# A decoder layer on one core: its second half recorded and emitted in a planned order, with three plain output pairs, fixed rings, one load queue and earlier gate columns

## The chip, the cores and the metric

The kernel runs on one core of one Trainium2 chip. A core has a matrix engine (PE, with a separate track PEld for its weight loads), a vector engine (DVE), a scalar engine (ACT), a general engine (POOL, used here only to issue transfers) and a queue engine (SP, which only issues transfers). The metric is the device time of one launch in microseconds (us), lower is better. The kernel before was run three times: 2223.91, 2223.79 and 2219.65 us, median 2223.79.

## The reference

One decoder layer for T = 512 tokens, width D = 2048, all inputs fp32. Cut to what matters here:

```python
mod = silu(c) @ W_ada + b_ada            # 6 groups of 16 columns of 128: shift1 scale1 gate1 shift2 scale2 gate2
h   = rms_norm(x) * (1 + scale1) + shift1
u   = h @ W_in                           # conv heads, queries, keys, values, gates
y   = [rms_norm(conv(u)) | rms_norm(attention(u))]
x   = x + gate1 * (y @ W_out)            # attention half of W_out: 8 blobs w_oa, 8 blobs w_oa2
h   = rms_norm(x) * (1 + scale2) + shift2
x   = x + gate2 * (relu(h @ W1)**2 @ W2) # D_FF = 8192
out = rms_norm(x)
```

Three facts follow. The norm of the second `h` needs every column of `x`, so nothing of `h @ W1` can start for a token before the whole output projection of that token is done. gate2 is first needed when `W2` products are added to `x`. The last norm needs every column of the last `x`.

## The kernel before, in words

**Number format.** Each fp32 operand is split in a high part and a rest, and one fp32 product becomes three matmuls (`mm3`, L92 to L95): weight high by token high (L93), weight high by token low (L94), weight low by token high (L95). A weight blob of 128x1024 fp32 (0.5 MB) is loaded by SP into the raw ring `rw` of 6 tiles (`raw_blob`, L790), its high part made by an ACT copy (L800) and its low part by a DVE subtract (L801) into the ring `hl` of 3 tiles (`hilo`, `hl_tile`). Token tensors are kept transposed, 128 channels by tokens.

**What orders the work.** All instructions go through a tile framework that schedules them when the kernel is built; each engine then runs its own list in that order. The first part of the kernel is pinned to its program order through `pin` (`keep_in_program_order`). From the output projection `w_oa` on, nothing is pinned and the framework's scheduler decides. Tiles come from rings whose owner is also decided there: a main pool of 29 slots (`slot`), 5 temporaries (`temp`), 2 accumulators (`accum`), and 8 PSUM banks of 512 fp32 (`bankf`).

**Gate and shift columns.** A column of `mod` is two 0.5 MB blobs of `W_ada`, each multiplied with silu(c) by one DVE instruction (`dot`, L132 to L134; `ada`, L142). 56 columns stand in a list `todo` (L254) that is worked off inside the projections and the attention. The last 8 columns of gate2 are done in the loop over the `w_oa` blobs: `ada(M_G2 * NK + 8 + k, raw_blob)`, 16 loads and 16 dots.

**Output projection.** The loop over `w_oa` takes 8 blobs, each into 8 banks, 512 tokens wide. Then the 8 blobs of `w_oa2` are kept split (`kept`, L834) and `late_out(hf)` (L848) computes 8 x 8 x 3 matmuls of 256 tokens for the low half of the tokens, later for the high half. `residual` (L812) adds the result to `x`, and `square_into` gathers the squares for the norm. `low_tokens` (L888) norms the low half and makes the token operands B1 and B2; `row_norm` (L168) and `high_tokens(q)` (L897) do the high half.

**First feed-forward matrix.** 32 output pairs `p`; one pair is two 128-channel outputs for 512 tokens, from four blobs of `w_f1`. It is computed by a seven-product Strassen-Winograd scheme: `operands` (L918) makes three new weight sums and splits seven operands; each product is a `run` (L941) of 24 matmuls of 256 tokens against one of seven token operands B1, U6, T5, B2, T7, B3, T4. `ff1(p)` (L971) combines the results with five DVE subtracts from PSUM, squares, makes the seven operands of the hidden activations and stores them to DRAM tensors `gd` (L1015 and L1019, on POOL). Between the output projection and the loop over the pairs, `ahead` (L962) does the B1 and B2 products of pairs 0 to 2, which need low tokens only, while the high tokens are made.

**Second matrix.** For each of 8 groups `f` the seven token operands are read back from `gd` (14 loads of 512 KB, L1121, on POOL); 4 groups `q` of four `w_f2` blobs each are multiplied in the same seven-product scheme. In the first group the residual `x` is also read back in eight loads (`residual_pairs`, L1082, on POOL). `update` (L1046), `final` (L1051) and `finish` (L1056) add to `x` and norm it; the last quarter `plain(3)` (L1091) is done with eight ordinary products so that the end can be norming one half while the other is computed.

The order of the region, as written:

```python
    late_out(0); low_tokens(); late_out(1)
    ahead(0, B1); row_norm(bankf, sacc, D, r2, 2, 4)
    ahead(1, B1); high_tokens(0); ahead(2, B1); high_tokens(1)
    ahead(0, B2); high_tokens(2); ahead(1, B2); ahead(2, B2); high_tokens(3)
    for p in range(32): ff1(p)
    for f in range(8):            # L1117: 14 token loads, then 4 (in the last group 3) groups of blobs
        ...
    plain(3)
```

Of the kernel before, what the change touches and what calls it, by code (L numbers as in the profile page):

```python
# [8 lines left out]
F32 = mybir.dt.float32  # L9
# [27 lines left out]
M_SH1, M_SC1, M_G1, M_SH2, M_SC2, M_G2 = range(6)  # L37


@with_exitstack  # L40
def hybrid_layer(ctx: ExitStack, tc: tile.TileContext, a, out):
# [126 lines left out]
    def row_norm(bank, square, width, dst, t0=0, t1=NQ):  # L168
        total = bank()
        for t in range(t0, t1):  # L170
            nc.tensor.matmul(total[:, t:t + 1], square[:, t * P:(t + 1) * P], ones[:, 0:1],
                             start=True, stop=True)
        row_bcast(bank, total[:, t0:t1], width, dst[:, t0 * P:t1 * P])
# [73 lines left out]
    for i in range(4):  # L247
# [7 lines left out]
        + [M_G2 * NK + k for k in range(8)]  # L255
# [526 lines left out]
    HT = T // 2  # L782
    LO, HI = slice(0, HT), slice(HT, T)
# [3 lines left out]
    def bankf():  # L787
        return psf.tile([P, T], F32, name="pf")

    def raw_blob(src):  # L790
        raw = ffp.tile([P, 1024], F32, name="rw", bufs=6)
# [3 lines left out]
    def hl_tile():  # L795
        t = ffp.tile([P, 2, 1024], F32R, name="hl", bufs=3)
        return t[:, 0], t[:, 1]

    def hilo(dst, src):
        nc.scalar.activation(dst[0], src, AF.Copy)  # L800
        nc.vector.tensor_tensor(out=dst[1], in0=src, in1=dst[0].bitcast(F32), op=OP.subtract)  # L801
        return dst
# [9 lines left out]
    def residual(ps, m, c):  # L812
        xm = x1[m // 2][:, m % 2, c]
        nc.vector.scalar_tensor_tensor(out=xm, in0=ps[:, c], scalar=col(M_G1, m), in1=xm,
# [8 lines left out]
    for k in range(8):  # L823
# [4 lines left out]
        ada(M_G2 * NK + 8 + k, raw_blob)  # L828
    for i in range(8):
        residual(pm[i], i, whole)  # L830
# [4 lines left out]
    for i in range(8):  # L835
        if i < 3:
            dst = hl_tile()
        elif i == 3:
            dst = [ffp.tile([P, 1024], F32R, name="sg", bufs=2) for _ in range(2)]
        elif i == 4:  # L840
            dst = [ffp.tile([P, 2, 2, HT], F32R, name="gt", bufs=3).rearrange("p a b c -> p (a b c)")
# [4 lines left out]
    pm = [bankf() for _ in range(8)]  # L846

    def late_out(hf):  # L848
        c = halves[hf]
        for i in range(8):  # L850
            wh, wl = kept[i]
            for k in range(8):
                s = slice(k * P, (k + 1) * P)
                mm3(pm[i][:, c], wh[:, s], wl[:, s], mixa[k][:, 0, c], mixa[k][:, 1, c], k == 0, k == 7)
            residual(pm[i], 8 + i, c)
# [31 lines left out]

    def low_tokens():  # L888
        row_norm(bankf, sacc, D, r2, 0, 2)
# [7 lines left out]
    def high_tokens(q):  # L897
        xs2 = [x1[2 * q], x1[2 * q + 1]]
        for j in range(2):
            normed(2 * q + j, 1)  # L900
        t5, t7 = temp((P, 2, HT), name="t5"), temp((P, 2, HT), name="t7")
        for j, x in enumerate(xs2):
            sub(t5[:, j], x[:, 0, LO], x[:, 0, HI])
            sub(t7[:, j], x[:, 0, HI], x[:, 1, HI])
        for i, t in ((T5, t5), (T7, t7)):
            tok[i][q] = tslot()
            tsplit(tok[i][q], t)
        u6, t4 = temp((P, 2, HT), name="u6"), temp((P, 2, HT), name="t4")
        tok[B3][q] = tslot()
        for j, x in enumerate(xs2):  # L910
            sub(u6[:, j], t5[:, j], x[:, 1, HI], OP.add)
            sub(t4[:, j], x[:, 1, LO], u6[:, j])
            split(tok[B3][q][:, j], x[:, 1, HI])
        for i, t in ((U6, u6), (T4, t4)):
            tok[i][q] = tslot()
            tsplit(tok[i][q], t)

    def operands(raw, only=None):  # L918

        a11, a21, a22, a12 = raw  # L920
        s1, s2 = [ffp.tile([P, 1024], F32, name="sg", bufs=2) for _ in range(2)]
        sub(s1, a21, a22, OP.add)
        sub(s2, s1, a11, OP.add)
        skip = only is not None
        if not skip:
            yield hilo(hl_tile(), a11)
        else:
            yield None
        yield hilo(hl_tile(), s2)
        yield hilo(hl_tile(), s1)  # L930
        if not skip:
            yield hilo(hl_tile(), a12)
        else:
            yield None
# [318 lines left out]
```

## Time and profile before

| | us |
|---|---|
| median of three runs | 2223.79 |
| the profiled execution | 2224.19 |
| its span, first to last instruction | 2222.4 |
| PE busy in it | 2131.6 |
| DVE busy | 1918.1 |
| ACT busy | 1008.2 |
| POOL busy | 193.6 |
| mean granted PE clock | 0.981 of full |

The profile is that of one execution. Its page gives busy times, the span in 40 slices, the chain of work that ended last, and groups of instructions by line and operands. A matmul's own duration (0.28 us for 256 tokens) overlaps its neighbours, so the pace of PE is read from the count in a stretch, not from the mean of one. The stages of the region that the change touches lie, in the span's time, at: `w_oa` 797 to 842.4, `late_out(0)` and most of `late_out(1)` 842.4 to 892.9, the way into the pairs 892.9 to 975, the pairs to 1559.8, the way into the second matrix to 1600, the groups `f` to 2140, the last quarters to 2206.95, and the end to 2222.4.

### The profile page before, as it was taken

The page shows a single profiled execution, that of the slowest core. Times are in us where ns is not written, and L with a number is a line of the kernel's source. Part 1 is how long each engine was busy: PE and PEld are TensorE (multiplying, and loading weights), DVE is VectorE, ACT ScalarE, POOL GpSimd, SP SyncE. Part 2 cuts the span into 40 slices and gives each one's busy share as a digit, 9 for nine tenths or more (in the row PEclk, how much of TensorE's full clock was granted, in tenths as well). Part 3 has the DMA queues.
Part 4 walks back from the last instruction along what each step waited for, and adds up shares of the span by engine and source line. Part 5 has one row for each costly group of instructions (what it writes and reads, how often), then busy time and mean ns, then how long its engine had stood idle before and what let it go on. Part 6 is the DMA issues. An engine that isn't in the chain of part 4 may idle for free.

```text
span 2222.4 us, 37637 instructions
## 1 busy us (share of the span) xinstructions
PE 2131.6 (96%) x14942; PEld 1969.9 (89%) x14942; DVE 1918.1 (86%) x2998; ACT 1008.2 (45%) x1468; POOL 193.6 (9%) x366
## 2 busy tenths in 40 slices
PE   6999989999999999799999999999899999999997
PEld 4777778898777779799999999999899999999996
DVE  8889978877496687999999999999799999999996
ACT  4431333222354435665666556666333333333353
POOL 0000000000000001021111111113211011011000
PEclk7999999999999999899999999999999999999998
DMA  8985686954211165276665666658865466366442
GB/s 343 336 323 180 237 313 256 356 216 180 86 39 57 57 266 185 81 233 209 199 196 195 199 211 196 201 190 283 296 241 195 157 237 233 119 237 235 151 146 95
DMA packets 143984, 453.61 MB, mean 204 GB/s; under 512 B 15809, under 2 KB 20161, under 8 KB 143809
## 3 DMA queue, kind: packets, MB, share of 16 engines
q1 hardware_dynamic: 91104, 322.22, 40.4%
q0 software_dynamic: 51616, 127.95, 17.2%
q8 instruction: 117, 1.92, 0.3%
q10 hardware_dynamic: 1088, 1.05, 0.1%
q14 instruction: 59, 0.48, 0.1%
HBM read 383.00 MB, written 68.16 MB: 203 GB/s over the span
## 4 chain that ended last, share of the span: by engine, by line
PE 75%; DVE 13%; ACT 5%; DMA 4%; issue 2%; SPq 0%; DVEq 0%; ACTq 0%; POOL 0%; POOLq 0%
PE pf L95 18%; PE pf L93 18%; PE pf L94 18%; PE ps L94 5%; PE ps L95 5%; PE ps L93 5%; DVE scr L134 3%; DVE wl L84 2%; DMA tk<-g 1%; DVE hl L801 1%; ACT wh L83 1%; PE pw L94 1%; PE pw L95 1%; PE pw L93 1%; PE pt L719 1%
## 5 line engine op out<-in xcount | busy, mean ns | idle before, releaser
L93 PE MATMUL pf<-tk,hl 128*128 128x256 f32 x3576 | 1008.0, 282 | 12.3 <-DMA tk<-g 6.0
L95 PE MATMUL pf<-tk,hl 128*128 128x256 f32 x3576 | 1005.5, 282 | 12.2 <-DVE hl L801 12.2
L94 PE MATMUL pf<-tk,hl 128*128 128x256 f32 x3576 | 1006.7, 282 | 1.3 <-DVE tk L872 1.3
L93 PEld LDWEIGHTS pf<-tk,hl 128*128 128x128 f32 x3576 | 678.2, 190 | 15.3 <-ACT hl L800 8.0
L95 PEld LDWEIGHTS pf<-tk,hl 128*128 128x128 f32 x3576 | 676.7, 190 | 14.8 <-DVE hl L801 14.7
L94 PEld LDWEIGHTS pf<-tk,hl 128*128 128x128 f32 x3576 | 677.0, 189 | 1.7 <-DVE tk L872 1.6
L800 ACT ACTIVATE hl<-rw 128x1024 fp32r<-128x1024 f32 x264 | 278.8, 1056 | 303.6 <-PE pf L95 254.9
L801 DVE TENSOR_TENSOR hl<-rw,hl 128x1024 fp32r<-128x1024 f32 x264 | 321.9, 1219 | 25.6 <-ACT hl L800 25.2
L800 ACT ACTIVATE hl<-sg 128x1024 fp32r<-128x1024 f32 x189 | 200.3, 1061 | 267.7 <-PE pf L95 242.9
L801 DVE TENSOR_TENSOR hl<-sg,hl 128x1024 fp32r<-128x1024 f32 x189 | 230.5, 1221 | 41.7 <-ACT hl L800 41.3
L134 DVE SCALAR_TENSOR_TENSOR scr<-wa,cs 128x1024 bf16<-128x1024 f32 x176 | 211.0, 1220 | 8.1 <-DMA wa<-in_w_ada 8.0
L83 ACT ACTIVATE wh<-raw 128x1024 fp32r<-128x1024 f32 (+1 forms) x105 | 110.8, 1059 | 221.0 <-PE ps L94 105.1
L84 DVE TENSOR_TENSOR wl<-raw,wh 128x1024 fp32r<-128x1024 f32 (+1 forms) x105 | 128.6, 1225 | 56.6 <-ACT wh L83 54.2
L875 DVE TENSOR_TENSOR sg<-sg,rw 128x1024 f32<-128x1024 f32 x126 | 153.5, 1219 | 0.9
L95 PE MATMUL ps<-h_m,wl 128*128 128x512 f32 x360 | 142.8, 397 | 2.5 <-DVE wl L84 2.4
L93 PE MATMUL ps<-h_m,wh 128*128 128x512 f32 x360 | 142.6, 396 | 2.4 <-ACT wh L83 1.2
L94 PE MATMUL ps<-h_m,wh 128*128 128x512 f32 x360 | 141.8, 394 | 0.0
L1049 DVE SCALAR_TENSOR_TENSOR x<-pf,mod,x 128x256 f32<-128x256 f32 x256 | 119.7, 479 | 17.9 <-PE pf L95 14.9
L93 PE MATMUL ps<-h,wh 128*128 128x512 f32 x280 | 113.2, 404 | 13.1 <-ACT wh L83 9.1
L95 PE MATMUL ps<-h,wl 128*128 128x512 f32 x280 | 113.7, 406 | 2.4 <-DVE wl L84 2.4
L94 PE MATMUL ps<-h,wh 128*128 128x512 f32 x280 | 113.3, 405 | 0.0
L1015 POOL DMA_DIRECT2D g<-gt x192 | 101.0, 532 | 86.4 <-DVE gt L872 81.2
(325 smaller groups left out, 2974.1 us busy)
## 6 DMA issues: line engine op xcount, KB each, us to landing
rw<-in_w_f SPq DMA_DIRECT2D x262, 512.0 KB, 4.3
wa<-in_w_ada SPq DMA_DIRECT2D x176, 512.0 KB, 6.2
tk<-g POOLq DMA_DIRECT2D x114, 512.0 KB, 8.1
g<-gt POOLq DMA_DIRECT2D x192, 256.0 KB, 5.0
raw<-in_w_conv SPq DMA_DIRECT2D x32, 512.0 KB, 6.6
raw<-in_w_kv SPq DMA_DIRECT2D x16, 512.0 KB, 5.4
raw<-in_w_cv SPq DMA_DIRECT2D x16, 512.0 KB, 4.5
raw<-in_cmp_w SPq DMA_DIRECT2D x16, 512.0 KB, 5.4
```

Source lines behind the costliest of these rows:

```text
L83: pin(nc.scalar.activation(wh[:, :cols], raw[:, :cols], AF.Copy))
L84: pin(nc.vector.tensor_tensor(out=wl[:, :cols], in0=raw[:, :cols], in1=wh[:, :cols].bitcast(F32), op=OP.subtract))
L93: pin(nc.tensor.matmul(ps, lh, rh, start=start, stop=False, skip_group_check=more))
L94: pin(nc.tensor.matmul(ps, lh, rl, start=False, stop=False, skip_group_check=more))
L95: pin(nc.tensor.matmul(ps, ll, rh, start=False, stop=stop, skip_group_check=more))
L134: pin(nc.vector.scalar_tensor_tensor(out=scr, in0=w, scalar=1.0, in1=cs[i].rearrange("p a b -> p (a b)"), op0=OP.mult, op1=OP.mult, accum_ ...
L719: nc.tensor.transpose(pt[:, r * P:(r + 1) * P], probs[b, r][:, kb * P:(kb + 1) * P], ident)
L800: nc.scalar.activation(dst[0], src, AF.Copy)
L801: nc.vector.tensor_tensor(out=dst[1], in0=src, in1=dst[0].bitcast(F32), op=OP.subtract)
L875: nc.vector.tensor_tensor(out=dst, in0=x, in1=y, op=op)
L1015: nc.gpsimd.dma_start(out=gd[p // 4][idx[j]][p % 4 // 2][:, p % 2], in_=g[:, j])
L1049: nc.vector.scalar_tensor_tensor(out=xm, in0=src, scalar=gate, in1=xm, op0=OP.mult, op1=OP.add)
```

## The change

1. **Recorded order.** A class `Order` stands in for `nc` from `w_oa` on. It records every call with its operands, derives dependences from their extents, and gives each instruction a cost. `emit` then keeps PE's program order except for instructions marked `floating` (the norms), works due times back from the products, and simulates the five engines to pick at each step the instruction that can start earliest, among equals the one due first. All instructions go out in the order of their simulated begins, pinned.
2. **Fixed rings.** Every ring of the region becomes a `cycle` over tiles taken once, so owners follow the recorded order. In the second matrix two of the five temporaries and the tile `spare` hold `base`.
3. **Gate columns.** All 16 gate2 columns stand in `todo`. The eight that left the `w_oa` loop are worked off in the query projections; of their 16 loads six stand on SP ahead of the first `w_oc` blobs.
4. **Late output projection.** Two blobs share one PSUM bank, so a half takes 4 banks and not 8.
5. **Three plain pairs.** Pairs 0, 1 and 2 are computed with eight ordinary runs each and not with seven: 12 runs on the low tokens, then 12 on the high tokens. `plan`, `makes` and `stay` fix which blob is split when; five of the 24 operands are kept from the low part, so 19 blobs are loaded and split. `results_of` combines with two PSUM adds for a pair and not five. `ahead` and `snapshot` go.
6. **High tokens.** `high_tokens` first makes T5 and B3 for all four quarters, then T7, U6 and T4. T5 has its sign turned, so the weight operand s1 is split with a minus (`hilo(..., minus)`).
7. **One load queue.** The token loads from `gd` and the loads of the residual move from POOL to SP. The stores stay on POOL.
8. **Finish.** `finish` becomes one function whose norm is `floating`.

The diff at its core:

```diff
+class Order:
+    RATE = 390e3
...
+    def emit(self):
...
+                for x in c:
+                    at = max(free[e], x.ready, wire - 2.0 if x.size else 0.0)
...
+                    key = (at, 0 if x.loose else 1, x.late, x.i)
...
+        for x in sorted(out, key=lambda x: (x.begin, x.i)):
+            self.tc.keep_in_program_order(x.call())
...
-        + [M_G2 * NK + k for k in range(8)]
+        + [M_G2 * NK + k for k in range(NK)]
...
+    nc = order = Order(tc, x1[0].tensor.tag, NMAIN)
+    rw = cycle([ffp.tile([P, 1024], F32, name="rw", bufs=6) for _ in range(6)])
+    hl = cycle([ffp.tile([P, 2, 1024], F32R, name="hl", bufs=3) for _ in range(3)])
...
+    banks = cycle([psf.tile([P, T], F32, name="pf") for _ in range(8)])
+    temps = cycle([temp() for _ in range(5)])
...
-    def hilo(dst, src):
+    def hilo(dst, src, minus=False):
+        if minus:
+            nc.scalar.activation(dst[0], src, AF.Copy, scale=-1.0)
+            nc.vector.scalar_tensor_tensor(out=dst[1], in0=src, scalar=-1.0, in1=dst[0].bitcast(F32),
+                                           op0=OP.mult, op1=OP.subtract)
...
-        ada(M_G2 * NK + 8 + k, raw_blob)
...
     def late_out(hf):
+        ps = []
         for i in range(8):
+            if i % 2 == 0:
+                ps.append(bankf())
...
-                mm3(pm[i][:, c], wh[:, s], wl[:, s], mixa[k][:, 0, c], mixa[k][:, 1, c], k == 0, k == 7)
+                mm3(ps[-1][:, halves[i % 2]], wh[:, s], wl[:, s], mixa[k][:, 0, halves[hf]],
+                    mixa[k][:, 1, halves[hf]], k == 0, k == 7)
...
+    def half_norm(hf, dst):
+        with floating():
+            row_norm(bankf, sacc, D, dst, 2 * hf, 2 * hf + 2)
...
+    NP = 3
+    plan = [(p, b, i, u, 0, i == B1) for p in range(NP)
+            for b, i, u in ((A11, B1, 0), (A21, B1, 1), (A12, B2, 0), (A22, B2, 1))]
...
+    def results_of(p):
+        xy, zv = [next(rw) for _ in range(2)]
...
+            sub(y[:, 1 - u], firsts[p, u], results[p, u][:, HI], OP.add)
...
     late_out(0)
+    half_norm(0, r2)
     low_tokens()
     late_out(1)
-    ahead(0, B1)
-    row_norm(bankf, sacc, D, r2, 2, 4)
...
-    for p in range(32):
+    for n in range(5):
+        make(n)
+    for n in range(12):
+        part(n)
+    half_norm(1, r2)
+    high_tokens()
+    for n in range(12, 24):
+        part(n)
+        if n in (17, 19, 23):
+            results_of({17: 2, 19: 0, 23: 1}[n])
+    for p in range(NP, 32):
         ff1(p)
...
     def finish(hf):
         c = halves[hf]
+        with floating():
+            ps = row_norm(bankf, sacc, D, rf, 2 * hf, 2 * hf + 2)
...
-            nc.gpsimd.dma_start(out=x1[k], in_=x1d[k])
+            nc.sync.dma_start(out=x1[k], in_=x1d[k])
...
-                nc.gpsimd.dma_start(out=tok[i][j], in_=gd[f][i][j])
+                nc.sync.dma_start(out=tok[i][j].bitcast(F32), in_=gd[f][i][j].bitcast(F32))
...
     plain(3)
+    order.emit()
```

More of the change, by code (lines that the diff above doesn't have):

```diff
@@ L920, in operands @@
+    def operands(raw, minus=False):
         a11, a21, a22, a12 = raw
[L921 removed]
+        s1, s2 = [next(sg["sums"]) for _ in range(2)]
         sub(s1, a21, a22, OP.add)
         sub(s2, s1, a11, OP.add)
[L924 to L928, printed above, removed]
[L929 to L934 removed]
+        yield hilo(hl_tile(), a11)
+        yield hilo(hl_tile(), s2)
+        yield hilo(hl_tile(), s1, minus)
+        yield hilo(hl_tile(), a12)
```

399 lines of the change are left out of this document (290 added, 109 removed).

## The prediction, as recorded before the changed kernel ran

> **What bounds the kernel now.** I read the page's busy times first, then the stages, then groups and waits in the stages that lose time.
>
> ```profile
> PE 2131.6 (96%) x14942; PEld 1969.9 (89%) x14942; DVE 1918.1 (86%) x2998; ACT 1008.2 (45%) x1468; POOL 193.6 (9%) x366
> PE 75%; DVE 13%; ACT 5%; DMA 4%; issue 2%; SPq 0%; DVEq 0%; ACTq 0%; POOL 0%; POOLq 0%
> ```
>
> PE is busy 96% of the span, so an order can only win what PE loses. The last line is the chain that ended last: 75% matmuls, 13% DVE. Where PE loses is told by stretches (columns: stretch, length, busy time and count of PE, PEld, DVE, ACT, POOL, granted clock, DMA share, GB/s):
>
> ```profile
> 520.00:590.00 70.00, 70.00 (x304) 56.73 (x303) 36.02 (x45) 24.72 (x33) 0.00 (x0) 1.00 0.26 91
> 797.00:842.40 45.40, 41.78 (x178) 33.33 (x179) 36.65 (x59) 12.42 (x15) 1.21 (x2) 1.00 0.87 336
> 842.40:892.90 50.50, 49.92 (x416) 49.32 (x414) 39.12 (x75) 29.11 (x62) 6.48 (x10) 1.00 0.46 162
> 892.90:975.00 82.10, 67.20 (x467) 63.48 (x467) 78.89 (x131) 49.95 (x83) 7.94 (x15) 0.88 0.44 143
> 975.00:1559.80 584.80, 584.80 (x4966) 584.80 (x4965) 537.82 (x717) 361.98 (x509) 116.73 (x222) 1.00 0.66 210
> 1559.80:1600.00 40.20, 31.80 (x247) 31.04 (x246) 29.05 (x39) 11.90 (x15) 9.95 (x19) 0.92 0.93 342
> 1600.00:2140.00 540.00, 540.00 (x4582) 540.00 (x4581) 498.71 (x692) 209.83 (x211) 51.07 (x95) 1.00 0.55 199
> 2140.00:2206.95 66.95, 62.82 (x513) 61.04 (x511) 57.26 (x102) 33.61 (x62) 0.00 (x0) 1.00 0.19 63
> 2206.95:2222.40 15.45, 2.07 (x9) 1.06 (x7) 7.45 (x15) 2.38 (x6) 0.00 (x0) 0.62 0.61 209
> ```
>
> The fifth row gives the pace: 584.8 / 4966 = 0.1178 us a 256-token matmul with PE never idle, so a run of 24 is 2.83 us. At that pace the 416 and 467 matmuls before 975 would take 49.0 and 55.0 us; they lose 1.5 and 27.1 us. Of the 27.1 PE stands still for 14.9; the rest is the clock of 0.88. In the same way 1559.8 to 1600 loses 40.2 - 29.1 = 11.1, and 2140 to 2206.95 loses 66.95 - 60.4 = 6.5. The two long middles lose nothing. So some 46 us can be won, and no more unless work goes.
>
> **The change part by part.** *Gate columns out of the w_oa loop.* Sixteen dots go:
>
> ```profile
> L134 DVE SCALAR_TENSOR_TENSOR scr<-rw,cs x16: 1218/1221/1227, 800.1 to 830.6; 128x1024 bf16<-128x1024 f32 x16
> L93 PE MATMUL pf<-mixa,hl 128*128 128x512 f32 x48 | 19.0, 395 | 2.2 <-ACT hl L800 2.2
> L95 PE MATMUL pf<-mixa,hl 128*128 128x512 f32 x48 | 19.0, 396 | 0.5 <-DVE hl L801 0.5
> L95 PE MATMUL pf<-mixa,wl 128*128 128x512 f32 x16 | 5.5, 402 | 1.3 <-DVE wl L84 1.3
> ...
> 783.58 17.46 SPq L792 DMA_DIRECT2D rw<-in_w_ada  x4
> ...
> raw<-in_w_q SPq DMA_DIRECT2D x16, 512.0 KB, 3.6
> ```
>
> They are 16 x 1.22 = 19.5 us of DVE. Moved to the query projections they meet 70 - 36 = 34 us of idle DVE in the row from 520 to 590, with a DMA share of 0.26, so they cost nothing there. The tightest place in the changed lists: one gate load on SP waits for PE, its dot stands ahead of the last query weight's rest on DVE, and the first w_oc blobs stand behind it on SP. Load, dot and rest are 3.6 + 1.22 + 1.22 = 6.0 us after that wait; PE has two more blobs to do by then, 48 of the matmuls that run at 70 / 304 = 0.23 us, 11 us. If that cover were gone it would cost up to 6. In the w_oa loop PE waited 2.2 us for the first split, whose blob stood behind the four gate loads on SP quoted last but one, and 0.5 us for its rest. The load now comes earlier, but its split tile lies on staging tiles that earlier products still read, so I take 1.0 of the 2.7 (bounds 0 and 3). **-1.0.**
>
> *From the output projection into the pairs (842.4 to 975).* The groups of PE that wait, and what DVE does there:
>
> ```profile
> L95 PE MATMUL pf<-tk,hl 128*128 128x256 f32 x159 | 48.8, 307 | 9.2 <-DVE hl L801 9.2
> L93 PE MATMUL pf<-tk,hl 128*128 128x256 f32 x162 | 50.0, 309 | 2.7 <-ACT hl L800 2.1 <-DVE gy L875 0.4
> L171 PE MATMUL pf<-ones,sacc 128*128 128x1 f32 x8 | 1.2, 255 | 1.7 <-DVE sacc L810 1.7
> L94 PE MATMUL pf<-tk,hl 128*128 128x256 f32 x162 | 48.8, 302 | 1.3 <-DVE tk L872 1.3
> ...
> L801 DVE TENSOR_TENSOR hl<-rw,hl 128x1024 fp32r<-128x1024 f32 x15 | 18.3, 1220 | 1.3 <-ACT hl L800 1.2
> L875 DVE TENSOR_TENSOR gy<-pf,gy 128x256 f32<-128x256 f32 x5 | 2.1, 419 | 0.0
> ```
>
> PE waits 9.2 us for weight rests, 2.7 for high parts, 1.7 for the norm's sums, 1.3 for tokens: DVE is the bound, with 39.1 + 78.9 = 118 us busy of 132.6. The plain pairs take DVE work off: 19 splits in place of 21 splits and 12 weight sums are 14 fewer at 1.22 = 17.1 us; two PSUM adds and not five, three times, are 9 at 0.42 = 3.8. DVE is left with about 98 us. They cost PE three runs more: 72 x 0.1178 = **+8.5**. PE then needs (49.0 + 55.0) + 8.5 = 112.5 us; DVE fits with 15 to spare. ACT loses two copies and was the bound nowhere. The half norm floats:
>
> ```profile
> 894.79 0.61 PE L171 MATMUL pf<-ones,sacc 128*128 128x1 f32 x4 [1.68 <-DVE sacc L810]
> ...
> 896.63 1.03 PE L197 MATMUL pf<-dg,ones 128*128 128x256 f32 x2
> ...
> 2206.92 0.28 PE L95 MATMUL pf<-tk,sg 128*128 128x256 f32 x1
> 2209.48 0.61 PE L1060 MATMUL pf<-ones,sacc 128*128 128x1 f32 x4 [2.28 <-DVE sacc L810]
> ```
>
> The sums waited 1.68 us with PE empty; in the changed program's list they stand 15 products (1.8 us) behind the last product of the late output projection. Today the sums start 2.56 us behind the last product at the very end (2206.92 to 2209.48), and at least 1.7 here, so up to 0.8 us of wait stays in each of two norms, and about as much at the broadcast. One new wait: the scratch of `results_of` takes two of the six raw tiles, so the second and third blob of the fourth pair may be late by up to one run, 2.8 us. Losses left: 3 us in the sum; the lower bound is 0, the upper 12 (the 9.2 us of weight rests and the new wait, all staying). 28.6 - 3 = **-25.6.**
>
> Four banks a half and the turned sign move no time: the minus keeps one ACT and one DVE instruction of the same width, under a PE that is never idle in the pairs; a DVE form slower by as much as the dot against the subtract (1221 against 1220) is nothing.
>
> *Into the second matrix (1559.8 to 1600).* The waits of 1540 to 1600, and POOL's list:
>
> ```profile
> PE pf L93 <- DMA tk<-g: 6.0, 2, 5.4
> POOL g L1019 <- DVE gb L90: 4.8, 1, 4.8
> PE pf L95 <- DVE hl L801: 2.4, 2, 2.0
> ...
> 1553.69 0.54 POOL L1019 DMA_DIRECT2D g<-gb  x1 [4.85 <-DVE gb L90]
> 1554.22 0.54 POOL L1121 DMA_DIRECT2D tk<-g  x1
> ...
> 1563.12 1.21 POOL L1121 DMA_DIRECT2D tk<-g  x2 [0.92 <-DMA tk<-g]
> ```
>
> POOL issues token loads between stores, and a store that waits for its split (4.85 us) holds the loads behind it; PE waited 5.4 us for one. On SP the loads pass the stores. They then share the queue with weight blobs, and on average the stage already moves 342 GB/s at a share of 0.93, so the transfers themselves could be late: 14 loads and eight residual loads of 512 KB are 11.5 MB, 34 us at that rate. Token slots come free from 17 us ahead of the turn, and not all seven operands are needed first; I leave 1 us (bounds 0 and 11.1). **-10.1.**
>
> *The groups f.* The seven turns between groups lost nothing while POOL carried the loads. POOL's waits, over the span, and the loads:
>
> ```profile
> POOL tk L1121 <- PE pf L95: 487.9, 51, 61.3
> rw<-in_w_f SPq DMA_DIRECT2D x262, 512.0 KB, 4.3
> tk<-g POOLq DMA_DIRECT2D x114, 512.0 KB, 8.1
> ```
>
> A token load waits for its slot, up to 61.3 us, and on POOL nothing hurried stood behind it. On SP weight blobs do. The planned list puts each load where its slot should be free and the six raw tiles cover 1.5 groups of four blobs, 29.7 us at 7 x 2.83 = 19.8 a group; I take **0**, and its other end is a rival.
>
> *The last quarters (2140 to 2206.95).* PE's waits there:
>
> ```profile
> ACT hl L800 <- DVE rw L875: 12.3, 2, 6.4
> PE pf L93 <- ACT hl L800: 3.4, 3, 1.3
> ```
>
> A weight sum reaches DVE late, ACT waits 6.4 us for it, and PE waits 3.4 us for high parts. Due times put such sums first; I take half of the 6.5 lost: **-3.5** (bounds -6.5 and +5, a wait of ACT's size passed to PE). Behind 2206.95 the chain of last square, sum, norm, scaling and stores stays: 0.
>
> **Sum**: -1.0 - 25.6 + 8.5 - 10.1 - 3.5 = -31.7. Span 2222.4 - 31.7 = 2190.7; 1.8 us lie around it (2224.19 against 2222.4), so 2192.5. The profiled execution is 0.4 above the median of the runs, so 2192 by the median.
>
> The clock matters to what waits are left. Between 892.9 and 975 PE stood 14.9 us and lost 27.1, 1.8 for each us. [...]
>
> **The rivals.** *Slower: the fixed lists fall out of step in the pairs and groups.* Today the long middles have slack that the framework's own order keeps. Ten pairs, 1200 to 1400:
>
> ```profile
> L801 DVE TENSOR_TENSOR hl<-rw,hl 128x1024 fp32r<-128x1024 f32 x41 | 50.1, 1221 | 3.7 <-ACT hl L800 3.7
> L801 DVE TENSOR_TENSOR hl<-sg,hl 128x1024 fp32r<-128x1024 f32 x30 | 36.6, 1221 | 7.2 <-ACT hl L800 7.2
> ```
>
> DVE is 92% busy (537.82 of 584.80) and waits 3.7 + 7.2 = 10.9 us for ACT in ten pairs. The planner prices a 1024-wide subtract at 1.13 us where it takes 1.22, so its list can put work ahead of a split that then is late by a little each time. The gain of 31.7 is gone when 60 pairs and groups lose 0.53 us each. If the 1.1 us that DVE waits per pair passed to PE, 60 x 1.1 = 66 us, the time is 2258. Against it: 1.6 us of slack per pair and a ring of three operands, 5.7 us ahead of PE. Chance 0.08. [...]
>
> *Slower: the one load queue.* A token load on SP whose slot is not yet free stops the blobs behind it; it decides when such a wait passes the 29.7 us cover, and at seven turns a wait like the 61.3 us seen on POOL costs 7 x (61.3 - 29.7) = 221 us, one of 36 us costs 7 x 6.3 = 44, which makes 2236. For it: POOL waited 487.9 us in 51 waits. Against: the loads are listed by when the slots free. Chance 0.05.
>
> *The way into the pairs keeps half its loss.* If late norms and scratch hold 11 us and more, with the clock: 2192 + 11 = 2203. For it: 19 loads and splits must be timed right against DVE's remaining 98 us. Chance 0.13. *The turn to the second matrix keeps its loss* since DMA is at 0.93 there: 2192 + 10 = 2202. Chance 0.10. *All of it goes*, the leftovers of 1 + 3 + 3 and the last of w_oa too: 2183. Chance 0.10. *The order does not do what it says*, each wait taking a new place at the old size: 2224, chance 0.04.
>
> **How the numbers follow.** The likeliest case, 2186 to 2198 about 2192, has 0.50. Faster takes 0.50 + 0.13 + 0.10 + 0.10 = 0.83; slower 0.08 + 0.05 and half of the last case, 0.15; same 0.02 (0.2%, about what a measurement of this kernel can tell from no change). The range leaves out the slower rivals and a little of the two partial cases together (2192 + 11 + 10 = 2213) and of the best: 2180 to 2214.
>
> **What would show it.** Right: about 116 us where 132.6 were between 842.4 and 975 with DVE below 90% and the clock near 1; a turn to the second matrix with PE waiting under 2 us and no POOL token load; PE never idle in the pairs. Wrong: PE waiting on weight rests in every pair, or on raw blobs at each turn of `f` with SP waiting on token slots; a wait of 3 us or more before the fourth pair.

## The result and the profile after

The changed kernel took 2209.98 us (median of four runs, 2207.75 to 2211.31) where the kernel before took 2223.85 in the same session: a ratio of 0.9941, 95% interval 0.9923 to 0.9958. It is 13.9 us faster. The forecast was 31.7 us faster; the sign was right, the time lies inside the range, and the gain is less than half of what was said.

The page of the changed kernel gives these totals and this chain that ended last. All instructions of the recorded region carry line 111, the line that records a call; the first part's lines have moved (L93, L94, L95 are L286, L287, L288, and L84 is L277).

```profile
span 2206.0 us, 37901 instructions
PE 2134.1 (97%) x15014; PEld 1975.4 (90%) x15014; DVE 1896.1 (86%) x2975; ACT 1007.3 (46%) x1469; POOL 128.2 (6%) x244
PE 81%; DVE 10%; DMA 4%; ACT 3%; issue 1%; SPq 0%; DVEq 0%; ACTq 0%
```

PE has its 72 more matmuls, DVE 22 us less work than the 1918.1 of before, as reckoned. The stretches of the changed kernel (columns as in the prediction):

```profile
788.60:800.00 11.40, 7.32 (x21) 5.44 (x20) 7.10 (x11) 2.68 (x4) 0.00 (x0) 0.70 0.40 144
800.00:843.60 43.60, 42.11 (x174) 33.35 (x173) 16.36 (x16) 14.79 (x16) 0.67 (x1) 0.96 0.44 155
843.60:892.40 48.80, 47.07 (x392) 46.35 (x391) 35.90 (x68) 27.07 (x58) 6.33 (x10) 1.00 0.42 152
892.40:964.00 71.60, 70.51 (x593) 69.83 (x592) 59.76 (x113) 49.53 (x89) 9.16 (x17) 1.00 0.46 151
964.00:985.00 21.00, 16.06 (x115) 15.56 (x114) 15.59 (x20) 9.17 (x13) 2.63 (x5) 0.84 0.53 167
985.00:1148.70 163.70, 162.98 (x1380) 162.60 (x1379) 149.38 (x198) 99.49 (x138) 29.55 (x56) 1.00 0.64 204
1148.70:1502.70 354.00, 354.00 (x3002) 354.00 (x3001) 323.87 (x431) 219.80 (x307) 64.93 (x123) 1.00 0.62 198
1502.70:1625.50 122.80, 119.92 (x1002) 119.75 (x1001) 109.30 (x148) 60.41 (x81) 14.75 (x28) 0.99 0.85 304
1625.50:2098.80 473.30, 473.30 (x4002) 473.30 (x4002) 435.84 (x596) 177.30 (x167) 0.00 (x0) 1.00 0.52 198
2098.80:2191.65 92.85, 92.85 (x784) 92.74 (x782) 89.18 (x157) 51.12 (x90) 0.00 (x0) 1.00 0.35 128
```

The reader is to see that the way into the pairs is now nearly full (70.51 of 71.60) but for one hole at 964 to 985, that the last quarters have none, and that a new hole stands at the very start of the `w_oa` stage, with the clock at 0.70.

To compare like with like I cut both traces at the same products: the first and last `w_oa` product, the last product of the late output projection, and then products counted from the last one (8776, 5776, 4776 and 776 before it), which are the same work in both. Times in us, each the difference of two starts in the trace's timeline; the last column is the kernel with four edits, told below.

```
stage                                  forecast   before    after   four edits
start to first w_oa product               0       793.2    788.6     790.9
w_oa                                     -1.0      49.1     54.9      47.5
late output projection          }       -17.1      47.7     48.9      46.3
way in, to 8776 before the last }                 263.7    256.3     247.5
3000 products of the pairs                0       353.4    354.1     354.5
1000 products, the turn                 -10.1     129.2    122.8     118.3
4000 products of the groups               0       471.7    473.3     473.1
last 776 products                        -3.5      98.9     92.7      92.6
end                                       0        15.5     14.5      14.8
```

The first row can't be put down to the change: the 1601st matmul, ahead of every instruction that the change touches, starts at 404.2 in the trace before and at 401.5 in the trace after, and over the experiments, with and without the moved gate columns, the first `w_oa` product starts anywhere from 788.6 to 791.7. So the profiled spans (16.4 us apart) show a little more than the medians (13.9). What is missing of the forecast lies mainly in three rows: `w_oa` 5.8 us longer and not 1.0 shorter, the way into the pairs with the late projection 6.3 shorter and not 17.1, the turn 6.4 and not 10.1. The last quarters gave 6.2 and not 3.5.

The waits of PE from `w_oa` to the last product, of the changed kernel:

```profile
PE pf L111 <- ACT hl L111: 7.3, 3, 3.4
PE pf L111 <- DVE wl L277: 4.1, 1, 4.1
PE pf L111 <- DVE hl L111: 2.0, 2, 1.5
PE pf L111 <- DVE x L111: 1.7, 3, 0.6
PE pf L111 <- ACT rw L111: 0.9, 2, 0.5
```

The longest of them have an experiment each below. The kernel before had 13.1 us for weight rests in twelve waits and 6.0 for token loads:

```profile
PE pf L95 <- DVE hl L801: 13.1, 12, 3.1
PE pf L93 <- ACT hl L800: 7.7, 6, 2.2
PE pf L93 <- DMA tk<-g: 6.0, 2, 5.4
```

### The profile page after: what moved, and what is told of

It is laid out like the page before. It is cut to its first block, busy times and chain, and to the rows that moved or that the text cites. A ratio compares the mean times of both kernels' runs of the same rounds, so it can differ in the third digit from the quotient of the medians.

```text
span 2206.0 us, 37901 instructions
## 1 busy us (share of the span) xinstructions
PE 2134.1 (97%) x15014; PEld 1975.4 (90%) x15014; DVE 1896.1 (86%) x2975; ACT 1007.3 (46%) x1469; POOL 128.2 (6%) x244
## 4 chain that ended last, share of the span: by engine, by line
PE 81%; DVE 10%; DMA 4%; ACT 3%; issue 1%; SPq 0%; DVEq 0%; ACTq 0%
PE pf L111 62%; PE ps L287 5%; PE ps L288 5%; PE ps L286 5%; DVE scr L327 3%; DVE wl L277 2%; ACT wh L276 1%; DMA wa<-in_w_ada 1%; PE pw L288 1%; PE pw L287 1%; PE pw L286 1%; PE pt L912 1%; DMA raw<-in_w_conv 1%; PE pv L286 1%; PE pv L287 0%
## 5 line engine op out<-in xcount | busy, mean ns | idle before, releaser
L111 PE MATMUL pf<-tk,hl 128*128 128x256 f32 x10704 | 1272.3, 282 | 9.0 <-ACT hl L111 6.3
L111 PEld LDWEIGHTS pf<-tk,hl 128*128 128x128 f32 x10704 | 1269.8, 189 | 10.4 <-ACT hl L111 6.7
L111 ACT ACTIVATE hl<-sg 128x1024 fp32r<-128x1024 f32 x180 | 191.0, 1061 | 260.0 <-PE pf L111 242.7
L327 DVE SCALAR_TENSOR_TENSOR scr<-wa,cs 128x1024 bf16<-128x1024 f32 x192 | 229.9, 1220 | 7.3 <-DMA wa<-in_w_ada 7.0
L111 DVE TENSOR_TENSOR hl<-sg,hl 128x1024 fp32r<-128x1024 f32 x151 | 184.7, 1223 | 36.3 <-ACT hl L111 36.2
L277 DVE TENSOR_TENSOR wl<-raw,wh 128x1024 fp32r<-128x1024 f32 (+1 forms) x105 | 128.7, 1226 | 41.0 <-ACT wh L276 40.2
L111 DVE SCALAR_TENSOR_TENSOR x<-pf,mod,x 128x256 f32<-128x256 f32 (+1 forms) x280 | 135.0, 488 | 19.0 <-PE pf L111 18.2
L111 DVE TENSOR_TENSOR sg<-sg,rw 128x1024 f32<-128x1024 f32 x120 | 146.1, 1218 | 0.0
L288 PE MATMUL ps<-h_m,wl 128*128 128x512 f32 x360 | 142.9, 397 | 2.4 <-DVE wl L277 2.4
L286 PE MATMUL ps<-h_m,wh 128*128 128x512 f32 x360 | 142.8, 397 | 2.1 <-ACT wh L276 1.9
L287 PE MATMUL ps<-h_m,wh 128*128 128x512 f32 x360 | 142.0, 394 | 0.0
L286 PE MATMUL ps<-h,wh 128*128 128x512 f32 x280 | 113.4, 405 | 12.3 <-ACT wh L276 8.8
L288 PE MATMUL ps<-h,wl 128*128 128x512 f32 x280 | 113.7, 406 | 2.5 <-DVE wl L277 2.4
L287 PE MATMUL ps<-h,wh 128*128 128x512 f32 x280 | 113.2, 404 | 0.0
L288 PEld LDWEIGHTS ps<-h_m,wl 128*128 128x128 f32 x360 | 67.8, 188 | 20.7 <-DVE wl L277 5.1
L111 DVE TENSOR_TENSOR sg<-rw 128x1024 f32<-128x1024 f32 x60 | 73.2, 1220 | 13.9 <-DMA rw<-in_w_f 11.5
L286 PEld LDWEIGHTS ps<-h_m,wh 128*128 128x128 f32 x360 | 67.8, 188 | 18.9 <-ACT wh L276 4.1
L287 PEld LDWEIGHTS ps<-h_m,wh 128*128 128x128 f32 x360 | 67.7, 188 | 15.5
```

Source lines behind the costliest of these rows:

```text
L111: x.i, x.eng, x.call = len(self.nodes), eng, (lambda: real(*args, **kw))
L277: pin(nc.vector.tensor_tensor(out=wl[:, :cols], in0=raw[:, :cols], in1=wh[:, :cols].bitcast(F32), op=OP.subtract))
L286: pin(nc.tensor.matmul(ps, lh, rh, start=start, stop=False, skip_group_check=more))
L287: pin(nc.tensor.matmul(ps, lh, rl, start=False, stop=False, skip_group_check=more))
L288: pin(nc.tensor.matmul(ps, ll, rh, start=False, stop=stop, skip_group_check=more))
L327: pin(nc.vector.scalar_tensor_tensor(out=scr, in0=w, scalar=1.0, in1=cs[i].rearrange("p a b -> p (a b)"), op0=OP.mult, op1=OP.mult, accum_ ...
```

## The experiments

### The written order of the first w_oa products

The start of the `w_oa` stage in PE's timeline, kernel before:

```profile
793.21 0.40 PE L93 MATMUL pf<-mixa,wh 128*128 128x512 f32 x1
...
796.17 0.39 PE L94 MATMUL pf<-mixa,wh 128*128 128x512 f32 x1
797.88 0.50 PE L95 MATMUL pf<-mixa,wl 128*128 128x512 f32 x1 [1.32 <-DVE wl L84]
...
799.61 0.39 PE L93 MATMUL pf<-mixa,wh 128*128 128x512 f32 x1
```

and after:

```profile
788.62 0.62 PE L111 MATMUL pf<-mixa,wh 128*128 128x512 f32 x2
793.33 0.79 PE L111 MATMUL pf<-mixa,wl 128*128 128x512 f32 x1 [4.08 <-DVE wl L277]
```

Before, the framework's scheduler had put 14 of the 16 products with the high part of the first blob ahead of the first with its rest (793.21 to 796.56); those of the last bank came behind seven products with the rest, at 799.61. The recorded order keeps the products as `mm3` writes them, so the third product needs the rest, which DVE makes behind the last steps of the attention's output. The experiment puts the high products ahead, for this one blob, and all 16 of them:

```diff
         for i in range(8):
             s = slice(i * P, (i + 1) * P)
-            mm3(pm[i], wh[:, s], wl[:, s], mixa[k][:, 0], mixa[k][:, 1], k == 0, k == 7)
+            if k:
+                mm3(pm[i], wh[:, s], wl[:, s], mixa[k][:, 0], mixa[k][:, 1], False, k == 7)
+            else:
+                nc.tensor.matmul(pm[i], wh[:, s], mixa[k][:, 0], start=True, stop=False)
+                nc.tensor.matmul(pm[i], wh[:, s], mixa[k][:, 1], start=False, stop=False)
+        if k == 0:
+            for i in range(8):
+                nc.tensor.matmul(pm[i], wl[:, i * P:(i + 1) * P], mixa[k][:, 0], start=False, stop=False)
```

> The changed kernel, but for the first w_oa blob the 16 products with the weight's high part go ahead of the eight with its rest, as the scheduler had them before. Theory: keeping the written order of the products puts a product with the rest third in the list, so PE waits 4.1 us for the rest and then runs some 3.4 us at half clock; with 16 products (3.7 us) ahead of it the wait and the slow clock go: the stretch from the first to the last w_oa product falls from 54.9 us to 49 to 50, the time from 2210 to about 2205. Rival: the splits of the next blobs bound the stage anyway, the wait only moves to them: 0 to 1.5 us, 2208.5 to 2210.

Measured: 2203.66 us (2201.03 to 2208.22), ratio to before 0.9914 [0.9899, 0.9928]. Its `w_oa` stage and PE's start in it:

```profile
789.70:837.20 47.50, 45.21 (x193) 35.59 (x192) 23.32 (x27) 17.28 (x20) 0.67 (x1) 1.00 0.52 176
...
789.65 3.88 PE L111 MATMUL pf<-mixa,wh 128*128 128x512 f32 x16
794.34 1.88 PE L111 MATMUL pf<-mixa,wl 128*128 128x512 f32 x7 [0.81 <-DVE wl L277]
```

The wait is 0.81 us and not 4.08, the clock of the stage is 1.00, and the stage is 47.5 us and not 54.9. That is 7.4 us, of which the waits for the rest are 3.3; the others come with the clock (0.70 and 0.96 in the two rows of the changed kernel). By the median it is 6.3. The theory holds; the waits for later splits did not grow (0.96 and 0.53 us stand in both).

The size is in part chance. Five of the runs below leave this stage as in the changed kernel and have the same wait of 4.07 to 4.08 us, and yet it takes 52.0, 52.3, 52.3, 55.0 and 55.1 us in them. The stage in the changed kernel, and in the run of the next section:

```profile
788.60:843.50 54.90, 49.33 (x192) 38.71 (x191) 23.35 (x27) 17.46 (x20) 0.67 (x1) 0.91 0.43 153
791.50:843.80 52.30, 46.73 (x193) 36.86 (x191) 23.33 (x27) 17.43 (x20) 0.67 (x1) 0.97 0.47 159
```

In the first the granted clock is 0.50 from 792.2 to 799.0, with PE at work for 5.7 us of it where the expectation has some 3.4, and again from 809.3 to 812.7 behind the waits of 0.96 and 0.53 us; in the second only from 796.2 to 799.6, 3.4 us, and the same two waits leave it at 1.00. So the written order costs this stage 4.5 to 7.6 us against 47.5, as the clock happens to fall.

### The scratch of the plain pairs

From 966.2 to 971.8 PE of the changed kernel waits twice; DVE ahead of it waits for a blob:

```profile
969.59 0.72 PE L111 MATMUL pf<-tk,hl 128*128 128x256 f32 x2 [3.43 <-ACT hl L111]
971.82 1.44 PE L111 MATMUL pf<-tk,hl 128*128 128x256 f32 x5 [1.51 <-DVE hl L111]
...
965.67 1.23 DVE L111 TENSOR_TENSOR sg<-rw 128x1024 f32<-128x1024 f32 x1 [4.43 <-DMA rw<-in_w_f]
```

```diff
-        xy, zv = [next(rw) for _ in range(2)]
-        x, y, z, v = [t[:, h * T:(h + 1) * T].rearrange("p (a b) -> p a b", a=2) for t in (xy, zv) for h in range(2)]
+        x, y, z, v = [temp((P, 2, HT), name="r") for _ in range(4)]
```

> The changed kernel, but the results of the three plain pairs are combined in four temporaries and not in two tiles of the raw ring. Theory: the scratch holds back the loads of the fourth pair's blobs; without it the waits of 3.4 and 1.5 us there and the half clock behind them go, about 7 us: 2203. Rival: the blobs are late because the stores of the results fill the DMA engines at that time (400 GB/s): the waits stay, 2209 to 2211. Second rival: the temporaries are then missing for T7, U6 and T4, and a wait of the same size takes the place: 2208 to 2213.

Measured: 2199.14 us (2198.95 to 2201.17), ratio 0.9893 [0.9878, 0.9908]. The stretch around the fourth pair and the whole way in:

```profile
892.60:1140.30 247.70, 246.61 (x2082) 245.94 (x2082) 225.14 (x331) 158.78 (x240) 41.34 (x78) 1.00 0.62 192
965.00:985.00 20.00, 20.00 (x171) 20.00 (x170) 17.80 (x25) 12.19 (x18) 2.63 (x5) 1.00 0.63 200
```

PE is full from 965 to 985 and the way in falls from 256.3 to 247.6 us, 8.7 less. Neither rival holds: POOL issues as many stores as in the changed kernel (x5 in both rows around 965 to 985, and 78 over the whole way in, which are 17 + 5 + 56 in the rows of the changed kernel), and the temporaries were not missed. The median moved by 10.8, 2.1 more than the stage. This trace has its `w_oa` stage, which the edit does not touch, 2.6 shorter than the changed kernel's (52.3 and 54.9, above), which would cover it.

### The load queue

```diff
-            nc.sync.dma_start(out=x1[k], in_=x1d[k])
+            nc.gpsimd.dma_start(out=x1[k], in_=x1d[k])
...
-                nc.sync.dma_start(out=tok[i][j].bitcast(F32), in_=gd[f][i][j].bitcast(F32))
+                nc.gpsimd.dma_start(out=tok[i][j], in_=gd[f][i][j])
```

> The changed kernel, but the token loads and the residual loads are issued by POOL again, in the planned order. Theory: the loads behind waiting stores made the loss at the turn to the second matrix; it comes back, from 5 to about 11 us: 2216. Rival: the planned order alone keeps the loads clear of the stores, the queue is indifferent: 2209 to 2211.

Measured: 2204.98 us (2204.12 to 2207.06), ratio 0.9919 [0.9903, 0.9936]: faster with POOL, against both. The turn, with the loads on POOL:

```profile
1504.80:1623.00 118.20, 118.20 (x1002) 118.20 (x1001) 109.32 (x148) 60.37 (x81) 34.47 (x65) 1.00 0.92 318
1530.00:1570.00 40.00, 40.00 (x341) 40.00 (x340) 36.59 (x52) 21.57 (x29) 15.62 (x29) 1.00 1.05 385
```

PE never stops. In the changed kernel it stopped for 2.88 us, until 1567.2, behind a weight sum that waited 4.79 for its blob. The first line is the stretch 1530 to 1570 there, the others the issues between 1540 and 1565 with the median time to landing:

```profile
1530.00:1570.00 40.00, 37.12 (x304) 36.95 (x303) 32.03 (x44) 18.92 (x25) 3.16 (x6) 0.96 1.01 381
...
1562.79 1.23 DVE L111 TENSOR_TENSOR sg<-rw 128x1024 f32<-128x1024 f32 x1 [4.79 <-DMA rw<-in_w_f]
...
rw<-in_w_f SPq DMA_DIRECT2D x5, 512.0 KB, 10.7
tk<-g SPq DMA_DIRECT2D x4, 512.0 KB, 13.6
```

Both move the same 381 to 385 GB/s. In the changed kernel the 19 loads that SP issued from 1535.57 to 1558.93 landed in the order of their issue, from 1542.34 to 1569.03, and the blob that DVE waited for, issued at 1551.98 and landed at 1562.70, stands behind token and residual loads that are due later; with POOL the blobs of that time landed in a median of 7.9 us:

```profile
rw<-in_w_f SPq DMA_DIRECT2D x6, 512.0 KB, 7.9
```

The planner lays out all lists anew when the queue changes, so the queue and its new list are shown together and not apart.

The same move alone, in the kernel before:

> The kernel before, with the token loads and the residual loads alone moved from POOL to SP. Theory: under the framework's own scheduler the loads on POOL stand behind waiting stores, so on SP the 11 us lost at the turn to the second matrix shrink to about 5, the size that they have with one queue in the planned order: 2217 to 2219. Rival: token loads that wait for a slot stop the weight blobs behind them on SP, at the turn and at each group: 2224 or more, by several us a group.

Measured: 2222.20 us (2219.03 to 2224.20), ratio 0.9990 [0.9981, 0.9999]. The turn takes 127.8 us where it took 129.2, with one wait of 7.40 us for a split in place of the waits for token loads; the groups take 471.7 as before. The 1.4 us are less than this stage differs by without an edit to it (131.4 in the run with the gate columns alone, below), so under the framework's scheduler the queue alone shows no gain there, while it costs 4.6 under the planned order. It was the planned order, not the queue, that took the loss out of the turn. The rival failed too: no weight blob was held up in the groups.

### The plain pairs

The changed kernel with the old scheme for pairs 0 to 2 (B1 and B2 products ahead, then seven products without those two), everything else kept:

```diff
-    for n in range(5):
-        make(n)
-    for n in range(12):
-        part(n)
+    for p in range(3):
+        ahead(p, B1)
     half_norm(1, r2)
     high_tokens()
-    for n in range(12, 24):
-        part(n)
-        if n in (17, 19, 23):
-            results_of({17: 2, 19: 0, 23: 1}[n])
-    for p in range(NP, 32):
+    for p in range(3):
+        ahead(p, B2)
+    for p in range(32):
         ff1(p)
```

> The changed kernel without the plain pairs: pairs 0 to 2 by the seven-product scheme, their B1 and B2 products ahead while the high tokens are made, as before the change, but in the planned order. Theory: the plain pairs took 21 us of DVE work out of the way into the pairs; without them PE saves 8.5 us of products but waits for DVE again for 15 to 20: 2216 to 2222. Rival: the planned order made the gain alone and the plain pairs only cost their 8.5 us: 2200 to 2204.

Measured: 2215.08 us (2211.79 to 2216.18), ratio 0.9960 [0.9945, 0.9975]. In this run the ring gave pair 2 its early bank a second time while its B1 and B2 products were still to be read, so that pair's values are other ones; the amount of work is the same. A second run has the norm recorded ahead of the early products, which moves the ring by two banks:

> As the run without the plain pairs, with the norm of the high half recorded ahead of the early products, so that no bank is taken while it is read. Theory: the norm's place among the products is found by the planner, so the time is as there, 2215, and PE still waits some 20 us for tokens and splits before the first pair. Rival: with the bank free the waits fall to the size that they have with the plain pairs, 10 us: 2203 to 2207.

Measured: 2216.86 us (2216.35 to 2218.38), ratio 0.9969 [0.9957, 0.9981]. Its way into the pairs and PE's waits there:

```profile
897.40:1000.00 102.60, 82.00 (x637) 79.63 (x636) 97.81 (x159) 62.58 (x101) 10.74 (x20) 0.87 0.47 148
...
PE pf L111 <- ACT tk L111: 15.5, 3, 12.2
PE pf L111 <- DVE tk L111: 2.6, 4, 1.2
PE pf L111 <- DVE t L111: 2.5, 2, 1.3
```

PE waits 15.5 us for the high tokens while DVE is busy 97.8 of 102.6 us. The planned order alone does not help here: the stage takes 264.2 us, against 263.7 in the kernel before. The plain pairs are what helps: with them 12 runs and not six lie between the low and the high tokens, and DVE has less to do. One thing was not tried: this run still makes T5 and B3 of all quarters ahead of U6, the order that suits the plain pairs. DVE's 97.8 of 102.6 us leave 4.8 us idle in this stretch, so another order of the tokens had little to win. The plain pairs are worth 6.9 us as built and 17.7 with the scratch out of the raw ring (2216.86 to 2199.14).

### The gate columns

Alone, in the kernel before:

```diff
-        + [M_G2 * NK + k for k in range(8)]
+        + [M_G2 * NK + k for k in range(NK)]
...
-        ada(M_G2 * NK + 8 + k, raw_blob)
```

> The kernel before, with the gate columns alone moved out of the w_oa loop into the query projections. Theory: 19.5 us of idle vector time and eight loads leave the w_oa stage, which lost about 5 us before; its waits of 1.5, 2.4 and 0.7 us shrink by 1 to 3 and the way into the pairs gains nothing: 2221 to 2223. Rival: the scheduler uses the freed vector time to split the later blobs ahead, and up to half of the 28 us lost on the way into the pairs goes: 2210 to 2214.

Measured: 2220.61 us (2215.83 to 2222.24), ratio 0.9983 [0.9973, 0.9992]; the `w_oa` stage takes 46.5 us and not 49.1, the way in 264.0 as before. And undone in the changed kernel, with the dots recorded in the `w_oa` loop:

> The changed kernel with the eight gate2 columns in the w_oa loop again, in the planned order. Theory: as in the kernel before, where moving them alone took 2.6 us off the w_oa stage, they cost some 2 to 3 us there, on top of the wait for the first rest: first to last w_oa product 57 to 58 us, time 2212 to 2213. Rival: the planner puts the dots, which are due only in the second matrix, behind all that is due earlier, so the w_oa stage stays at 52 to 55 and the time at 2209 to 2211; a second: they move into the way into the pairs, where vector time is short, and that stage grows by several us, 2214 or more.

Measured: 2219.02 us (2213.95 to 2221.29), ratio 0.9973 [0.9963, 0.9983]. The `w_oa` stage and the late projection:

```profile
790.70:849.20 58.50, 49.63 (x193) 38.44 (x191) 36.74 (x60) 13.11 (x14) 0.00 (x0) 0.91 0.69 244
849.20:906.40 57.20, 50.17 (x391) 48.76 (x390) 42.58 (x75) 31.28 (x64) 7.02 (x11) 0.94 0.48 173
```

They take 12.0 us more than in the changed kernel (54.9 + 48.9), part of it at the lower clock of 0.91 and 0.94. The theory is too small; the time is where the second rival had it, but the loss lies in the late projection (57.3 us) and not in the way into the pairs (258.5 against 256.3). The planner takes what can start earliest; four dots in a row, due only in the second matrix, start at 810.8 to 814.3, a split waits behind them, PE waits 2.80 us for it, and later PE waits 4.75 for a residual. So the gate columns are worth 2.9 us by themselves and some 9 under the planned order, whose rule would let them in the way.

### The late output projection's banks

```diff
-            if i % 2 == 0:
-                ps.append(bankf())
+            ps.append(bankf())
```

with one blob to a bank, in its low half.

> The changed kernel with eight banks a half in the late output projection, one blob to a bank, and no other edit. Theory: where two blobs share a bank, PE stops 0.58 us in the second blob until the vector engine has read the first, three times; with a bank each the three waits go, the late output projection takes 46.3 us and not 48.9, the time is about 2207.5. Rival: the bank ring then runs out for the early products and a wait of the same size comes behind it: 2209 to 2211.

Measured: 2204.96 us (2203.31 to 2208.26), ratio 0.9915 [0.9900, 0.9930]. The stage, first with shared banks and the engines' waits for each other there, then with a bank each:

```profile
852.90 0.48 DVE L111 SCALAR_TENSOR_TENSOR x<-pf,mod,x 128x256 f32<-128x256 f32 x1 [0.17 <-PE pf L111]
853.44 0.99 PE L111 MATMUL pf<-mixa,sg 128*128 128x256 f32 x6 [0.58 <-DVE x L111]
```

```profile
845.80:892.10 46.30, 46.30 (x392) 46.20 (x391) 35.92 (x68) 26.41 (x58) 6.01 (x10) 1.00 0.46 161
```

The three waits are gone and the stage takes 46.3 us and not 48.9. With a shared bank the program holds PE's products for one half until DVE's read of the other half is done: the wait of 0.58 us ends with the semaphore of that DVE instruction. What the bank would do without this order, no run here shows. The rival's wait behind it did not come; the way into the pairs takes 256.2 us, against 256.3 in the changed kernel. The median moved by 5.0 where the stage explains 2.5; the other stages of its trace are those of the changed kernel within 1.3 us. That trace is of the slowest of its four runs, and the changed kernel's is of the fastest of its four, so I put the rest down to the spread of the runs.

### The four edits together

> The changed kernel with four edits at once: the high products of the first w_oa blob ahead of its rests, the results of the plain pairs in temporaries, the loads on POOL again, and the late output projection in eight banks a half, one blob to a bank, as before the change. Theory: the four losses are apart in time and add up by stage: 7.4 (first to last w_oa product) + 8.7 (way into the pairs) + 4.6 (turn to the second matrix) + 2.2 (three waits of 0.74 in the late output projection): 2210 - 23 = 2187. Rival: an earlier PE only meets the same splits and loads later, as in the front, where earlier starts were given back: two thirds of it, 2193 to 2197.

Measured: 2187.26 us (2186.35 to 2189.22), ratio to before 0.9836 [0.9820, 0.9853], 22.7 us below the changed kernel and 36 below the kernel before. The stretches, cut at the same products as above:

```profile
790.90:838.40 47.50, 45.19 (x192) 35.52 (x191) 23.32 (x28) 17.31 (x21) 0.97 (x2) 1.00 0.53 176
838.40:884.70 46.30, 46.30 (x391) 46.20 (x390) 36.00 (x68) 26.75 (x59) 6.05 (x10) 1.00 0.46 161
884.70:1132.20 247.50, 246.55 (x2081) 245.89 (x2080) 225.47 (x331) 159.06 (x240) 41.35 (x78) 1.00 0.62 192
1132.20:1486.70 354.50, 354.50 (x3002) 354.50 (x3001) 324.17 (x431) 219.83 (x307) 64.90 (x123) 1.00 0.65 198
1486.70:1605.10 118.40, 118.40 (x1003) 118.40 (x1003) 109.41 (x149) 60.51 (x81) 34.54 (x65) 1.00 0.91 312
1605.10:2078.20 473.10, 473.10 (x4003) 473.10 (x4002) 434.63 (x596) 177.31 (x167) 43.80 (x82) 1.00 0.58 199
```

The four losses add up: 7.4 + 2.5 + 8.8 + 4.5 = 23.2 us by stage (the two spans are 20.5 us apart, since this trace comes to `w_oa` 2.3 later). This version beats both kernels. Its PE waits about 3 us in all between the first `w_oa` product and the last product.

### The pace of the products

Where PE never waits, a product takes 0.1183 us in the groups of the changed kernel (473.3 / 4002) and 0.1179 before (540.0 / 4582, from the prediction's row). I asked whether the place of the instructions sets it:

> The four edits together, and the first w_oa product is issued twice, the second overwriting the first: one more 512-token matmul, 0.23 us. It asks why PE's pace in the second matrix is 0.1183 us a product in the changed kernel and 0.1179 in the kernel before with no wait in either. Theory: the pace hangs on where the instructions lie, so shifting all later ones by one changes the 473.1 us of those 4000 products by 0.5 us or more. Rival: it hangs on the lists themselves: 473.0 to 473.3.

Measured: 2187.38 us, a single run; the 4000 products took 473.1 us again. So a shift by one instruction does not do it. The run without the plain pairs has 471.8 us there with the same number of products, so the planned order as such does not do it either. The 1.5 us to the changed kernel's 473.3 stay unexplained.

## Why the prediction was right or wrong

**The stages named were the right ones, and the two middles held.** The gains that came lie where the prediction put them, apart from `w_oa`; DVE's work fell by the amount reckoned, and the three extra runs cost what they should (in the run with the scratch in temporaries the 2082 products of the way in kept PE busy for 246.61 us, 0.1184 each, 8.5 for 72). The rival that the fixed lists fall out of step failed: no wait of PE stands in the 3000 products of the pairs or in the 4000 of the groups; what they lost is 0.6 and 1.6 us of pace. The rival with token loads stopping the blobs by tens of us failed too.

**The step of the w_oa stage failed in sign.** It looked at the wait for the loads and for DVE's dots, forecast -1.0, and the stage gave +5.8 in the profiled run (+2.9 to +6.0 over the six traces with this order). It took the order of the products for given. That PE keeps its written order stands in the description of the change, and the row quoted (1.3 us waited for `wl`) stood for an order that the scheduler had turned: 14 high products, 3.4 us, hid most of the rest's delay. The prediction's stage starts at 797, and the first `w_oa` product at 793.2, so its rows do not show them. What the fixed order removes there was never priced. With that one blob turned the stage took 47.5. The term itself had the right sign: alone, the gate columns took 2.6 us off the stage.

**The new wait in the raw ring was seen and mis-sized.** "Up to one run, 2.8 us", counted in the leftovers of 3 in the term of -25.6, measured 3.43 + 1.51 us of waiting, and 8.7 with the clock behind it. I had sized it by one run of PE. In the trace four blobs were issued within 4.1 us, from 954.25 to 958.32, and took 4.3, 5.9, 6.3 and 7.3 us to land: DVE had the one it needed, the last of them, only at 965.6. The wait for the norm's sums ahead of the pairs, on the other hand, is 0.15 us (at 896.9) and not 0.8.

**The turn's gain had the wrong owner.** "On SP the loads pass the stores" was the reason given for -10.1. The planned order brings -11 by itself with the loads on POOL (118.2 us), and the one queue, with the list made for it, gives 4.6 back. The sentence that they share the queue with weight blobs was there, with the DMA share of 0.93 beside it; it should have been a term of the sum and not its bound.

**Shared banks "move no time" was wrong by 2.5 us.** No row of before shows PE writing one half of a bank while DVE reads the other; it was priced at nothing without a cover being named.

**The last quarters were better than said.** -6.2 and not -3.5: due times took all of the four waits there, not half.

**The clock.** The prediction has a rate, 1.8 us lost for each us of waiting, but its sum puts no clock on the 3 us of leftovers. Around the waits of 4.08, 3.43 and 2.88 us the profile shows 0.70, 0.84 and 0.96 in the rows of 788.6, 964 and 1530 (0.50 from 792.2 to 799.0, from 969.7 to 976.5 and from 1567.1 to 1570.4), while the three waits of 0.58 us in the late output projection left the clock at 1.00. The rate was about right: 4.9 us of waits at the fourth pair cost 8.7. How long a wait was did not tell by itself whether the clock fell: behind the waits of 0.96 and 0.53 us in `w_oa` it fell in three of the six traces and not in the others.

**The sum.** -31.7 was forecast and -13.9 came: 6.8 us of difference from `w_oa`, 10.8 from the way in with the late projection (mostly the scratch, 8.7, and the banks, 2.5), 3.7 from the turn, 2.2 from the pace, against 2.7 and 1.0 better at the last quarters and the end. That makes -11.8 for the change's own stages; the two traces add 4.6 in the front, of which 2.7 stand ahead of every changed instruction, and the medians lie between.

## What to carry to other kernels

When a scheduler's list is replaced by a written one, read what the old list had quietly turned: a product that needs a late operand may have been moved behind those that don't, and a fixed order takes that cover away. Price a scratch tile in a load ring by when the loads behind it land together (here four were issued within 4.1 us and the last took 7.3 us to land), and a merged queue by what is issued earlier and due later. And undo each detail alone: here four of them cost 23 us under a change that won 14.

## What was not expected of the hardware

In the changed kernel a wait of 2.88 us ends at 1567.2, and the granted clock was 0.50 from 1567.1 to 1570.4 and 0.96 over the 40 us from 1530 to 1570. The price of the same wait differed: with the stop of 4.07 to 4.08 us in `w_oa` the clock of 0.50 lasted 6.8 us in the changed kernel and 3.4 in the run with the scratch in temporaries, and over the six traces the stage took 52.0 to 55.1 us with the same instructions. The pace of 256-token products that wait for nothing differed by 0.3% between lists (0.1179 to 0.1183 us); the 4000 products of the groups took 473.3 us in the changed kernel and in three of the experiments alike, and no cause was found.
